# A transformer decoder layer on one core: new durations in the count of times that places the steps of a top-k search

## The chip, the cores and the metric

The kernel runs on one core of one Trainium2 chip. The metric is the device time of one execution in microseconds (us). The kernel before takes 1329.95 us, the median of three runs (1328.74 to 1334.31).

## What is computed

One decoder layer on 1024 tokens of 1024 channels. The steps that matter here, cut from the reference:

```
h    = x * (1 + scale1) + shift1                       # scale, shift, gate from c @ W_mod
q, k, v, u, iq, ik, iw = split(h @ W_in)
score = sum over 8 indexer heads of iw * relu(iq . ik / 8), causal
idx   = top_k(score, 256)                              # per query, the 256 best keys
attn  = softmax attention of 8 heads over the keys idx only
pool  = causal window means (2, 4, 8, 16) of u, minus u, then a small matmul
x = LayerNorm(alpha * x + gate1 * (concat(attn, pool) @ W_o))
x = LayerNorm(alpha * x + gate2 * SwiGLU(x * (1 + scale2) + shift2))
```

Queries are worked on in eight tiles of 128 (tile 0 to tile 7). Tile i looks at 128 (i + 1) keys. Tiles 0 and 1 have at most 256 keys and need no selection.

## The kernel before, in words

The layer runs in stages: modulation and indexer projection, indexer scores (tiles 2 to 7 in turn), projections of u (pooling), k and v, attention, W_o with the first norm, and the feed-forward part.

**The search.** The 256th best score of a row is found by bisection over the bits of the score (`bisect`). A search has a first pass over the score, then 15 steps on the high 16 bits (`search_v` or `search_a` with `bits` 15), a pass that prepares the low bits, 16 steps on the low bits, and last a few operations that turn the found threshold into a mask written over the score. Three searches run side by side. One is on VectorE, for tiles 7, 6 and 5 at once (`TILES_V`; its small columns are `colsD`, its keys `keysD` and `keys`, its waste output `junk`): one step is three counting passes of 1024, 896 and 768 elements and two tiny operations. Two are on ScalarE: one for tiles 4 and 3 (`junkA`), one for tile 2 (`junkB`), with columns `colsA`; their first passes, their change from high to low bits and their masks are on VectorE too.

**The projections beside it.** While the searches run, TensorE computes u in four groups (`u_take` copies a group from PSUM on ScalarE into `ub` and forms the window sums on VectorE and GpSimd, `u_split` forms `phi` on ScalarE and `plo` on VectorE, `u_pool` multiplies), then k in eight tiles (`take` copies on ScalarE and rotates on GpSimd, `k_transpose` transposes on TensorE into `kT`, copies the high part on ScalarE and subtracts the low part on VectorE, both into `kr`), then v in eight tiles. Weights of each are split into a high and a low part (`ws`): high on ScalarE, low on VectorE for two quarters and on GpSimd for the other two. `gate_fin` (`gr`) stands in the middle of v.

**Attention.** It goes from tiles 7 and 6 down. A unit is a pair of heads of one tile: scores on TensorE (`s`, from `kr` and the query operands `qab`), mask and row maximum on VectorE (`sm`, in the trace CUSTOM_DVE_ANT_0, in the order of the program ISA), exponential on ScalarE, reciprocal on VectorE, scaling on GpSimd, transposes on TensorE (`pT`), product with v (`o`). `need(i)` makes sure that the mask of tile i has been issued before its first use.

**What sets the order.** Engines run their own queues in order. In the stages with the search, VectorE, ScalarE and GpSimd keep the order in which the program issues (`PIN`). That order is made by a count of times: each engine is wrapped in a `Queue`, which adds the assumed duration of each instruction (`cost`) to its own clock and notes when each buffer is written and read (`Times`). Before an instruction goes out, `fill` asks when its operands would be ready; if a waiting search step with its announced duration (the number after `yield`) ends by then plus a slack of 0.3 us (VectorE) or 0.4 us (ScalarE), the step goes out first. Steps that found no place are issued when `need` asks for the mask. No assumed duration reaches the chip except through this order. Behind the projections, VectorE, ScalarE and TensorE are ordered by the framework's scheduler, which does not read these durations.

Of the kernel before, what the change touches and what calls it, by code (L numbers as in the profile page):

```python
# [131 lines left out]
class Queue:  # L132
# [6 lines left out]
    def cost(self, op, out, k):  # L139
        n = 1  # L140
        for s_ in out.shape[1:]:
            n *= s_
        if self.name == "T":
            return 0.107 if op == "transpose" else max(n, 60) / 2400
        if self.name == "A":
            return max(0.19, 0.05 + n * 0.00088) + (0.09 if "accum_out" in k else 0)
        if self.name == "G":
            return 0.12 + n * {"tensor_tensor": 0.00225, "scalar_tensor_tensor": 0.0014}.get(op, 0.00125)
        if out.dtype in (BF16, I16, U16) and op in ("tensor_scalar", "tensor_tensor", "tensor_copy"):
            return 0.07 + n * (0.00065 if "accum_out" in k or op == "tensor_tensor" else 0.0003)  # L150
        return 0.07 + n * (0.00053 if op == "tensor_scalar" else 0.00106)

    def __getattr__(self, op):
        f = getattr(self.eng, op)
# [26 lines left out]
def decoder_layer_kernel(  # L181
# [8 lines left out]
    V, A, G, T, SP = (Queue(tc, e, n, pinned, times) for e, n in  # L190
                      ((nc.vector, "V"), (nc.scalar, "A"), (nc.gpsimd, "G"), (nc.tensor, "T"), (nc.sync, "S")))
# [448 lines left out]
    def bisect(tiles, cols, on_act):  # L640

        nt = len(tiles)
# [6 lines left out]
        def trash(i):  # L649
            return (ja if on_act else junkd(i))[:, 0 : P * (i + 1)]  # L650
# [10 lines left out]
        for m, i in enumerate(tiles):  # L661
            n = P * (i + 1)
# [8 lines left out]
        sum_w = sum(w_(i) for i in tiles)  # L671

        def search_v(bits, base, low):
            V.memset(cand, float(1 << (bits - 1)))
            for b in range(bits - 1, -1, -1):
                yield "V", 0.35 + 0.72 * sum_w
                for m, i in enumerate(tiles):
                    dt = U16 if low else I16
                    V.tensor_scalar(trash(i).bitcast(dt), kv[i].bitcast(dt), one(cand, m), one(base, m),
                                    ALU.is_ge, ALU.add, accum_out=one(cntc, m))  # L680
                V.tensor_scalar(pr, cntc, 0.0, float(1 << b), ALU.is_ge, ALU.mult)
                off = -float(1 << (b - 1)) if b > 0 else -1.0
                V.scalar_tensor_tensor(cand, pr, off, cand, ALU.add, ALU.add)

        def search_a(bits, low):

            V.memset(cand, 0.5 - float(1 << (bits - 1)))
            for b in range(bits - 1, -1, -1):
                yield "A", 1.0 * sum_w + 0.65 * nt
                for m, i in enumerate(tiles):  # L690
                    A.activation(trash(i), kv[i].bitcast(U16 if low else I16), AF.Sign, bias=one(cand, m),
                                 accum_out=one(cntc, m))

                for m in range(nt):
                    A.activation(one(pr, m), one(cntc, m), AF.Sign, bias=one(thr, m))
                for m in range(nt):
                    A.activation(one(cand, m), one(pr, m), AF.Identity, scale=-0.5 * float(1 << b), bias=one(cand, m))
            yield "V", 0.1
            V.tensor_scalar(cand, cand, -1.0, None, ALU.mult)

        yield from (search_a(15, False) if on_act else search_v(15, kp, False))
        V.tensor_copy(M, cand)
        for m, i in enumerate(tiles):
            yield "V", 1.8 * w_(i)
            V.tensor_scalar(trash(i).bitcast(I16), kv[i], one(M, m), one(kp, m), ALU.is_gt, ALU.add,
                            accum_out=one(ng, m))
            lv = score(i).bitcast(U16).rearrange("p (n two) -> p n two", two=2)
            V.scalar_tensor_tensor(kv[i].bitcast(U16), kv[i], one(M, m), lv[:, :, 0], ALU.is_equal, ALU.mult)
            if on_act:
                V.tensor_scalar(one(thr, m), one(ng, m), 2.0, float(P * (i + 1) + 1), ALU.mult, ALU.add)  # L710
        yield from (search_a(16, True) if on_act else search_v(16, ng, True))

        V.tensor_copy(ib.bitcast(I32), M)
# [4 lines left out]
        for m, i in enumerate(tiles):  # L718
            n = P * (i + 1)
# [66 lines left out]
    for i in range(2, NT):  # L786
# [3 lines left out]
        n = P * (i + 1)  # L790
# [970 lines left out]
    for p in range(1, NFP):  # L1761
        n_of = {"g": 0, "d": 0, "u": 0}
        for kind in DOWN_AT if p < NFP - 1 else "g" * 7 + "u" * 7:
            n = n_of[kind]
# [134 lines left out]
```

## Time and profile before

| what | value |
|---|---|
| median of three runs | 1329.95 us |
| the profiled execution | 1327.57 us, its span 1325.8 us |
| mean granted TensorE clock | 0.955 |
| TensorE (PE) busy | 1186.7 us, 90% |
| VectorE (DVE) busy | 1070.5 us, 81% |
| ScalarE (ACT) busy | 642.7 us, 48% |
| GpSimd (POOL) busy | 709.2 us, 53% |

Shares over the whole span mix stages with different limits. The searches lie between about 126 and 415 us of the span, so the stretches of that time have to be read one by one. All instructions of wrapped engines carry line 168, which is a helper's, so rows are told apart by the names of their buffers.

### The profile page before, as it was taken

To read this page: it belongs to the slowest core of one execution; us is meant where nothing else is said; L and a number is where in the kernel's file an instruction comes from. 1 tells how busy PE (TensorE), PEld (TensorE's weight loads), DVE (VectorE), ACT (ScalarE), POOL (GpSimd) and SP (SyncE) were. 2 spreads that over 40 slices of the span, in tenths; PEclk is the share of its full clock that TensorE was granted. 3 is DMA by queue.
4 is the path that set the end of the run, shared out by engine and by line. 5 is a ranking of instruction groups with operands and counts; after the bars stand their busy time and mean duration, and the time that the engine had idled before them with its cause. 6 is when DMAs were issued, how large, how long until landed. Compare 5 with 4: busy or idle time off the path is not lost.

```text
span 1325.8 us, 16034 instructions
## 1 busy us (share of the span) xinstructions
PE 1186.7 (90%) x5462; PEld 927.9 (70%) x5462; DVE 1070.5 (81%) x1769; ACT 642.7 (48%) x1335; POOL 709.2 (53%) x495
## 2 busy tenths in 40 slices
PE   7979996858749997999689999999999999999996
PEld 6646585646536654788577787878787887878775
DVE  6898999999997698576687787776868777777698
ACT  3345794847857776535544343333334333333531
POOL 1392463535003354428677384765748475576848
PEclk9999998979878998999899999999999999999998
DMA  9540020301100166420020101102120111113113
GB/s 341 225 158 26 17 96 17 111 33 48 41 16 9 57 215 239 148 84 9 32 96 32 64 33 64 64 32 80 39 73 32 64 36 61 64 47 112 43 60 120
DMA packets 34904, 103.91 MB, mean 78 GB/s; under 512 B 3843, under 2 KB 3843, under 8 KB 33286
## 3 DMA queue, kind: packets, MB, share of 16 engines
q1 hardware_dynamic: 34822, 102.88, 22.3%
q8 instruction: 43, 0.70, 0.2%
q14 instruction: 39, 0.32, 0.1%
HBM read 93.42 MB, written 9.45 MB: 78 GB/s over the span
## 4 chain that ended last, share of the span: by engine, by line
PE 37%; DVE 6%; POOL 4%; issue 2%; ACT 1%; DVEq 0%; POOLq 0%; ACTq 0%
PE gu L168 23%; PE dn L168 14%; DVE act_W L168 2%; POOL wraw_R L168 2%; DVE utmp_X L168 1%; POOL wraw_W L168 1%; DVE gtmp_V L168 1%; POOL wblk_V L168 1%; POOL wblk_T L168 0%; DVE wblk_T L168 0%; DVE hr_H L168 0%; POOL hr_H L168 0%; DVE wblk_V L168 0%; DVE res_X L168 0%; DVE stat_C L168 0%
## 5 line engine op out<-in xcount | busy, mean ns | idle before, releaser
L168 PE MATMUL gu<-hr_H,wblk_V 128*128 128x512 f32 (+1 forms) x924 | 215.7, 385 | 4.3 <-POOL wblk_V L168 2.1
L168 PE MATMUL gu<-hr_H,wblk_T 128*128 128x512 f32 (+1 forms) x924 | 215.6, 385 | 3.6 <-POOL wblk_T L168 1.9
L168 PEld LDWEIGHTS gu<-hr_H,wblk_V 128*128 128x128 f32 x924 | 169.9, 188 | 41.3 <-POOL wblk_V L168 4.2
L168 PEld LDWEIGHTS gu<-hr_H,wblk_T 128*128 128x128 f32 x924 | 170.5, 188 | 39.9 <-POOL wblk_T L168 3.6
L168 DVE TENSOR_TENSOR res_X<-res_X,dn 128x512 f32<-128x512 f32 (+1 forms) x253 | 158.9, 677 | 15.4 <-PE dn L168 15.3
L168 POOL TENSOR_SCALAR sm_H<-sm_H,stat_X 128x1024 f32<-128x1024 f32 (+7 forms) x64 | 57.2, 907 | 139.0 <-DVE stat_X L168 127.8
L168 PE MATMUL pj<-ws_W,hT_H 128*128 128x512 f32 x456 | 122.0, 416 | 10.5 <-DVE kr_K L168 5.4
L168 POOL TENSOR_TENSOR wraw_R<-wraw_R 128x512 f32<-128x512 f32 x64 | 94.3, 1481 | 47.0 <-DVE wblk_T L168 23.7
L168 POOL TENSOR_TENSOR wraw_W<-wraw_W 128x512 f32<-128x512 f32 x60 | 86.7, 1452 | 57.9 <-DVE wblk_V L168 29.3
L168 PEld LDWEIGHTS pj<-ws_W,hT_H 128*128 128x128 f32 x456 | 87.0, 197 | 37.7 <-issue 15.5
L168 PE MATMUL dn<-wblk_T,act_W 128*128 128x512 f32 x324 | 78.8, 391 | 4.5 <-DVE act_W L168 4.5
L168 PE MATMUL dn<-wblk_V,act_W 128*128 128x512 f32 x324 | 78.5, 391 | 2.9 <-DVE act_W L168 2.5
L168 DVE TENSOR_SCALAR_CACHE_REDUCE junk_X<-keysD_T,colsD_X 128x1024 int16<-128x1024 int16 (+1 forms) x64 | 78.9, 1269 | 0.7
L168 ACT ACTIVATE wblk_V<-wraw_R 128x512 fp32r<-128x512 f32 x56 | 35.3, 630 | 81.0 <-POOL wraw_R L168 62.6
L168 PEld LDWEIGHTS dn<-wblk_T,act_W 128*128 128x128 f32 x324 | 60.4, 188 | 19.0 <-DVE act_W L168 6.6
L168 PEld LDWEIGHTS dn<-wblk_V,act_W 128*128 128x128 f32 x324 | 60.4, 188 | 17.4 <-DVE act_W L168 4.2
L168 ACT ACTIVATE wblk_V<-wraw_W 128x512 fp32r<-128x512 f32 x53 | 33.1, 628 | 75.0 <-POOL wraw_W L168 56.4
L168 ACT ACTIVATE wblk_T<-wraw_W 128x512 fp32r<-128x512 f32 x56 | 35.0, 628 | 65.9 <-POOL wraw_W L168 50.2
L168 POOL TENSOR_TENSOR ws_W<-raw_R,ws_W 128x1024 fp32r<-128x1024 f32 x11 | 30.8, 2797 | 63.2 <-ACT ws_W L168 63.2
L168 ACT ACTIVATE wblk_T<-wraw_R 128x512 fp32r<-128x512 f32 x52 | 32.5, 627 | 60.9 <-POOL wraw_R L168 45.5
L168 POOL TENSOR_TENSOR ptmp_C<-rope_V,gr_G 128x512 f32<-128x512 f32 x16 | 25.8, 1610 | 66.1 <-ACT rope_V L168 65.7
L168 ACT ACTIVATE sm_H<-sm_H,stat_X 128x1024 f32<-128x1024 f32 (+7 forms) x64 | 49.1, 768 | 23.4 <-DVE stat_X L168 23.1
(298 smaller groups left out, 2785.6 us busy)
## 6 DMA issues: line engine op xcount, KB each, us to landing
wm_K<-in_wma_dram SPq DMA_DIRECT2D x16, 512.0 KB, 9.9
modraw_V<-in_wmc_dram SPq DMA_DIRECT2D x16, 512.0 KB, 4.5
wraw_R<-in_wg_dram SPq DMA_DIRECT2D x6, 1024.0 KB, 4.7
wraw_R<-in_wd_dram SPq DMA_DIRECT2D x12, 512.0 KB, 3.6
wraw_W<-in_wup_dram SPq DMA_DIRECT2D x12, 512.0 KB, 3.6
modraw_V<-in_wmg_dram SPq DMA_DIRECT2D x10, 512.0 KB, 4.3
wraw_R<-in_wup_dram SPq DMA_DIRECT2D x10, 512.0 KB, 3.5
wraw_W<-in_wg_dram SPq DMA_DIRECT2D x5, 1024.0 KB, 4.7
```

The costliest lines, as they stand in the source:

```text
L168: ins_ = f(*a, **k)
```

## The change

The assumed durations of instructions on TensorE, ScalarE and VectorE are replaced, and so are the announced durations of a search step. For the VectorE search (three tiles, summed width 2.625) a step was announced as 0.35 + 0.72 * 2.625 = 2.24 and is now announced as 0.4 + 1.08 * 2.625 + 0.35 * 3 = 4.29. No instruction is added or taken away and no operand changes; the order of VectorE, ScalarE and TensorE changes, that of GpSimd and of the DMA queue does not.

```diff
         if self.name == "T":
-            return 0.107 if op == "transpose" else max(n, 60) / 2400
+            return 0.13 if op == "transpose" else max(n * 0.000443, 0.11)
         if self.name == "A":
-            return max(0.19, 0.05 + n * 0.00088) + (0.09 if "accum_out" in k else 0)
+            return max(0.26, 0.14 + n * 0.00088) + (0.31 if "accum_out" in k else 0)
...
         if out.dtype in (BF16, I16, U16) and op in ("tensor_scalar", "tensor_tensor", "tensor_copy"):
-            return 0.07 + n * (0.00065 if "accum_out" in k or op == "tensor_tensor" else 0.0003)
-        return 0.07 + n * (0.00053 if op == "tensor_scalar" else 0.00106)
+            if "accum_out" in k:
+                return 0.35 + n * 0.00105
+            return 0.07 + n * (0.00065 if op == "tensor_tensor" else 0.0003)
+        return max(0.16, 0.07 + n * (0.00053 if op == "tensor_scalar" else 0.00106))
...
-                yield "V", 0.35 + 0.72 * sum_w
+                yield "V", 0.4 + 1.08 * sum_w + 0.35 * nt
...
-                yield "A", 1.0 * sum_w + 0.65 * nt
+                yield "A", 0.9 * sum_w + nt
```

**First place: VectorE where the first key tiles get their low parts.** `kr` is the key operand, `kT` the transposed key tile in PSUM, `junk` with `colsD` a search step. In the kernel before:

```order
L168 TENSOR_SCALAR junk_X_607,colsD_X_615<-keysD_T_610,colsD_X_615 128x1024
L168 TENSOR_SCALAR junk_X_608,colsD_X_615<-keysD_T_610,colsD_X_615 128x896
L168 TENSOR_SCALAR junk_X_609,colsD_X_615<-keys_T_612,colsD_X_615 128x768
L168 TENSOR_SCALAR colsD_X_615<-colsD_X_615 128x3
L168 SCALAR_TENSOR_TENSOR colsD_X_615<-colsD_X_615 128x3
L168 TENSOR_TENSOR kr_K_1231<-kT_1990,kr_K_1231 64x4x128 x2
L168 TENSOR_TENSOR kr_K_1231<-kT_2021,kr_K_1231 64x4x128 x2
```

The same place in the changed kernel, with the ScalarE searches' change to the low bits (`colsA`, `keysA`) and the next weight split:

```order
L170 TENSOR_TENSOR kr_K_1225<-kT_1849,kr_K_1225 64x4x128 x2
L170 TENSOR_SCALAR junkA_T_613,colsA_X_606<-keysA_X_605,colsA_X_606 128x512
L170 SCALAR_TENSOR_TENSOR keysA_X_605<-keysA_X_605,colsA_X_606,score_X_77 128x512
L170 TENSOR_SCALAR colsA_X_606<-colsA_X_606 128x1
L170 MEMSET colsA_X_606 128x2
L170 TENSOR_TENSOR kr_K_1225<-kT_1924,kr_K_1225 64x4x128 x2
L170 TENSOR_TENSOR kr_K_1225<-kT_1946,kr_K_1225 64x4x128 x2
L170 TENSOR_TENSOR kr_K_1225<-kT_1990,kr_K_1225 64x4x128 x2
L170 TENSOR_TENSOR ws_W_69<-raw_R_75,ws_W_69 128x1024
```

The search steps that stood between the key tiles before are gone from between the first four.

**Second place: VectorE around the gate row in the middle of v.** `gr` is the gate, `gt` its PSUM tile. In the kernel before:

```order
L168 TENSOR_SCALAR junk_X_607,colsD_X_615<-keysD_T_610,colsD_X_615 128x1024
L168 TENSOR_SCALAR junk_X_608,colsD_X_615<-keysD_T_610,colsD_X_615 128x896
L168 TENSOR_SCALAR junk_X_609,colsD_X_615<-keys_T_612,colsD_X_615 128x768
L168 TENSOR_SCALAR colsD_X_615<-colsD_X_615 128x3
L168 SCALAR_TENSOR_TENSOR colsD_X_615<-colsD_X_615 128x3
L168 TENSOR_TENSOR gr_G_76<-raw_R_73,gt_2386 128x512
L168 TENSOR_TENSOR gr_G_76<-raw_R_73,gt_2399 128x512
```

The same place in the changed kernel; the rows that write `keysD` and `keys` from `score` are the search's change from high to low bits:

```order
L170 TENSOR_TENSOR gr_G_76<-raw_R_73,gt_2266 128x512
L170 SCALAR_TENSOR_TENSOR keysD_T_610<-keysD_T_610,colsD_X_615,score_X_77 128x1024
L170 TENSOR_TENSOR gr_G_76<-raw_R_73,gt_2274 128x512
L170 TENSOR_SCALAR junk_X_608,colsD_X_615<-keysD_T_610,colsD_X_615 128x896
L170 TENSOR_SCALAR junk_X_609,colsD_X_615<-keys_T_612,colsD_X_615 128x768
L170 SCALAR_TENSOR_TENSOR keysD_T_610<-keysD_T_610,colsD_X_615,score_X_77 128x896
L170 SCALAR_TENSOR_TENSOR keys_T_612<-keys_T_612,colsD_X_615,score_X_77 128x768
L170 MEMSET colsD_X_615 128x3
```

Before, 29 of the 31 steps stand ahead of the gate and 2 behind it; now 15 stand ahead of it and all 16 steps on the low bits behind it, along with most of the preparation of the low bits.

**Third place: VectorE at the first attention unit.** ISA is the masked row maximum of a head. In the kernel before:

```order
L168 TENSOR_SCALAR keys_T_611<-score_X_77,colsA_X_606 128x640
L168 TENSOR_SCALAR junkA_T_613,colsA_X_606<-score_X_77,colsA_X_606 128x640
L168 TENSOR_SCALAR keysA_X_605<-score_X_77,colsA_X_606 128x512
L168 TENSOR_SCALAR colsA_X_606<-colsA_X_606 128x1
L168 TENSOR_TENSOR qab_H_2528<-qT_2535,qab_H_2528 64x512
L168 SCALAR_TENSOR_TENSOR score_X_77<-keys_T_611,colsA_X_606 128x640
L168 TENSOR_TENSOR qab_H_2528<-qT_2535,qab_H_2528 64x512
L168 TENSOR_SCALAR score_X_77<-score_X_77 128x640
L168 TENSOR_TENSOR qab_W_2529<-qT_2540,qab_W_2529 64x512 x2
L168 ISA sm_H_2527,stat_X_2522<-s_2619,score_X_77 128x1024
```

And in the changed kernel:

```order
L170 TENSOR_SCALAR score_X_77<-junk_X_607 128x1024
L170 TENSOR_SCALAR keys_T_611<-score_X_77,colsA_X_606 128x640
L170 TENSOR_SCALAR junkA_T_613,colsA_X_606<-score_X_77,colsA_X_606 128x640
L170 TENSOR_SCALAR keysA_X_605<-score_X_77,colsA_X_606 128x512
L170 TENSOR_SCALAR colsA_X_606<-colsA_X_606 128x1
L170 ISA sm_H_2390,stat_X_2385<-s_2452,score_X_77 128x1024
L170 ISA stat_X_2385 128x1
L170 SCALAR_TENSOR_TENSOR score_X_77<-keys_T_611,colsA_X_606 128x640
```

The masks of tiles 7, 6 and 5 were complete ahead of the first ISA; now only that of tile 7 is, the ends of the others follow between the ISA rows of the first units, and the four operations on `qab` stand earlier, among the low steps.

## Rows read from the trace of the kernel before

**Rows 1.** Stretches: length, busy us (instructions) of PE, PEld, DVE, ACT, POOL, clock, DMA:
```profile
189.60:369.40 179.80, 133.92 (x546) 106.01 (x545) 173.04 (x318) 118.27 (x332) 57.98 (x39) 0.88 0.15 50
369.40:394.70 25.30, 9.57 (x36) 6.06 (x34) 24.74 (x46) 13.99 (x37) 0.00 (x0) 0.67 0.07 21
394.70:430.00 35.30, 33.25 (x177) 21.49 (x178) 28.93 (x65) 26.00 (x54) 12.81 (x12) 0.80 0.03 8
```
**Rows 2.** Timeline of DVE: start us, us, operation, idle before it:
```profile
202.73 1.34 DVE L168 TENSOR_SCALAR_CACHE_REDUCE junk_X<-keysD_T,colsD_X 128x1024 int16<-128x1024 int16 x1
...
206.63 1.34 DVE L168 TENSOR_SCALAR_CACHE_REDUCE junk_X<-keysD_T,colsD_X 128x1024 int16<-128x1024 int16 x1
...
216.66 1.22 DVE L168 TENSOR_TENSOR plo_V<-ub_V,phi_V 128x1024 fp32r<-128x1024 f32 x1 [1.12 <-ACT phi_V L168]
...
229.35 1.23 DVE L168 TENSOR_TENSOR plo_V<-ub_V,phi_V 128x1024 fp32r<-128x1024 f32 x1 [1.13 <-ACT phi_V L168]
...
244.47 2.85 DVE L168 TENSOR_TENSOR ub_V<-ub_V 128x1024 f32<-128x1024 f32 x1 [0.50 <-ACT ub_V L168]
247.66 1.23 DVE L168 SCALAR_TENSOR_TENSOR ub_V<-ub_V,ub_V 128x1024 f32<-128x1024 f32 x1 [0.34 <-POOL ub_V L168]
```
**Rows 3.** Timeline of PE: start us, us, operations, idle before them:
```profile
172.83 11.12 PE L168 MATMUL pair<-hT_H,ws_W 128*128 128x512 f32 x48
...
217.16 1.22 PE L168 MATMUL po<-phi_V,wps_X 128*128 128x512 f32 x2 [11.46 <-ACT ub_V L168]
...
292.09 1.09 PE L168 MATMUL kT<-const_C,rope_V 128*128 128x128 f32 x4 [15.76 <-DVE kr_K L168]
...
326.14 5.61 PE L168 MATMUL pj<-ws_W,hT_H 128*128 128x512 f32 x24
...
361.14 12.68 PE L168 MATMUL pj<-ws_W,hT_H 128*128 128x512 f32 x48 [2.71 <-DVE gr_G L168]
...
404.78 3.67 PE L168 MATMUL pT<-const_C,sm_H 128*128 128x128 f32 x16
```
**Rows 4.** Timeline of ACT:
```profile
188.77 0.81 ACT L168 ACTIVATE junkA_T<-keys_T,colsA_X 128x640 bf16<-128x640 int16 x1
...
191.17 0.81 ACT L168 ACTIVATE junkA_T<-keys_T,colsA_X 128x640 bf16<-128x640 int16 x1
...
215.57 1.06 ACT L168 ACTIVATE phi_V<-ub_V 128x1024 fp32r<-128x1024 f32 x1 [15.85 <-DVE ub_V L168]
...
293.22 1.19 ACT L168 ACTIVATE kr_K<-kT 64x512 fp32r<-64x512 f32 x2 [13.36 <-PE kT L168]
```
**Rows 5.** Timeline of POOL:
```profile
198.60 6.35 POOL L168 TENSOR_TENSOR ub_V<-ub_V 128x1024 f32<-128x1024 f32 x3 [7.74 <-DVE ub_V L168]
...
237.16 2.87 POOL L168 TENSOR_TENSOR ws_W<-raw_R,ws_W 128x1024 fp32r<-128x1024 f32 x1 [3.18 <-ACT ws_W L168]
```
**Rows 6.** Timeline of DVE at the end of the search:
```profile
369.41 0.17 DVE L168 CAST colsD_X<-colsD_X 128x3 int32<-128x3 f32 x1
...
393.24 1.39 DVE L168 TENSOR_TENSOR qab_W<-qT,qab_W 64x512 fp32r<-64x512 f32 x2
394.66 1.23 DVE L168 CUSTOM_DVE_ANT_0 sm_H<-s,score_X 128x1024 f32<-128x1024 f32 x1
```
**Rows 7.** DVE groups from 189.5 to 369.4: count, busy us, mean ns, idle before:
```profile
L168 DVE TENSOR_TENSOR ws_W<-raw_R,ws_W 128x1024 fp32r<-128x1024 f32 x4 | 8.8, 2202 | 0.1
L168 DVE TENSOR_SCALAR colsD_X<-colsD_X 128x3 f32<-128x3 f32 (+1 forms) x32 | 8.7, 271 | 1.0
L168 DVE TENSOR_TENSOR ub_V<-ub_V 128x1024 f32<-128x1024 f32 x4 | 6.5, 1629 | 0.5 <-ACT ub_V L168 0.5
...
L168 DVE TENSOR_TENSOR plo_V<-ub_V,phi_V 128x1024 fp32r<-128x1024 f32 x4 | 4.9, 1221 | 2.3 <-ACT phi_V L168 2.2
```
**Rows 8.** Timeline of ACT and of DVE in the indexer scores:
```profile
144.04 0.61 ACT L168 ACTIVATE junkB_X<-keysA_X,colsA_X 128x384 bf16<-128x384 int16 x1 [3.11 <-DVE colsA_X L168]
...
163.63 2.67 DVE L168 SCALAR_TENSOR_TENSOR score_X<-relu_K,const_C,score_X 128x1024 f32<-128x1024 f32 x2 [0.55 <-ACT relu_K L168]
167.36 3.53 DVE L168 SCALAR_TENSOR_TENSOR score_X<-relu_K,const_C,score_X 128x1024 f32<-128x1024 f32 x2 [1.05 <-ACT relu_K L168]
```

## The prediction

> **What bounds the kernel now.** I first read the busy time by stretch, since shares of the whole span say little here. From 189.6 to 369.4 us, where the VectorE search runs beside the projections, VectorE is busy 173.0 of 179.8 us and TensorE 133.9 [rows 1]. So VectorE is the bound of that stretch and TensorE follows it. TensorE's timeline says the same from the other side: its long waits there, 11.46 us ahead of the first pooling product, 15.76 us ahead of the third key transpose and 2.71 us ahead of the last v tiles, all end with VectorE (the first by way of ScalarE's `phi`, which waits 15.85 us for VectorE) [rows 3, 4]. VectorE's own timeline shows how little it waits: four waits of 1.12, 1.13, 0.50 and 0.34 us, 3.1 us in all; the rest of the gap to 179.8 are short pauses between dependent tiny operations [rows 2]. The search ends at 369.41, the masks follow, and the first softmax operation starts at 394.66 [rows 6]. From 394.7 on TensorE is busy 33.25 of 35.3 us [rows 1]: the bound changes over to TensorE there. The time at which attention gets going is therefore set by VectorE: by the work that stands ahead of it, which is the same set of instructions in both kernels, plus VectorE's waits.
>
> **The change part by part.** A step of the VectorE search takes 3.90 us (206.63 minus 202.73) [rows 2]. Counted in the order, 29 of 31 steps stood ahead of the gate row and now 15 do. So 14 steps, 14 x 3.90 = 54.6 us, leave the projections and stand behind them, where nothing else is left for VectorE. For TensorE that is a gain: a group of 24 matmuls takes 5.61 us and 48 take 11.12 us [rows 3], and with its VectorE waits gone it should end the projections about 50 us earlier, near 322 instead of 373.8 us (361.14 + 12.68) [rows 3]. That gain is worth nothing by itself, since attention then stands still until the search is done. What counts is whether VectorE still has no waits while it paces nobody. It does not: with fewer steps to fill in, it waits for the others.
>
> I walked VectorE's new order from 189.6 us with the durations of the rows, against TensorE's, ScalarE's and GpSimd's new orders. The waits I find, with what ends them:
> - pooling, first group: 1.1 us for `phi`, as in the row before [rows 2].
> - second group: ScalarE now has three steps of its two-tile search (2.40 us each, 191.17 minus 188.77 [rows 4]) and the copies of the pooling product ahead of `phi`, so VectorE waits 2.7 us for it, and 0.4 us for GpSimd's sums.
> - first quarter of the k weights: one ScalarE step lies ahead of the copy, 2.0 us.
> - last two pooling groups: 0.3 us behind a GpSimd weight split of 2.87 us [rows 5] and 0.8 us for `phi`.
> - k tiles 0 to 3 have no step between them any more: VectorE needs 0.7 us for each half tile (1.39 for two such operations [rows 6]), TensorE 5.61 us for a tile's projection, ScalarE 1.19 us for the copy ahead of it [rows 3, 4]. Waits of 0.4 and 2.8 us.
> - k tiles 4 to 7, with the wait for the one-tile search's ScalarE part: 1.3, 2.5, 2.8 and 0.9 us.
> Sum: 1.1 + 3.1 + 2.0 + 1.1 + 3.2 + 7.5 = 18.0 us, against 3.1 us before. The ends of this term: 8 us if ScalarE and TensorE run ahead of my walk by a step each time, 25 us if each wait is a ScalarE step longer.
>
> Four operations on `qab`, 0.69 us each [rows 6], move from behind the search into it: +2.8 us for the search's end, and the same less behind it.
>
> Collisions with GpSimd take from this. The same kind of operation takes 1.22 us where GpSimd is quiet (`plo`) and 2.20 and 1.63 us on the mean for the weight splits and the window sums; the tiny `colsD` operation takes 0.27 us on the mean [rows 7] against 0.17 for the like one at the search's end [rows 6]. That excess is 4 x 0.98 + 4 x 0.41 + 32 x 0.10 = 8.8 us, with the like on other tiny operations some 11. GpSimd's work is unchanged, and in my walk two of its four weight splits meet VectorE again. I take 4 us as saved, out of a range from 0 to 11. The Trainium skill weighs in here: its page "SBUF — State Buffer", section "SBUF: two separate sides", says that a VectorE operation with two SBUF inputs and a GpSimd operation contend for one port pair, an exclusive lock, so that the loser is held for the other's whole instruction. By that rule a VectorE operation that starts during a 2.87 us split waits up to all of it, or not at all if it starts elsewhere; the rows agree in kind (2.85 us for one sum instead of 1.22 [rows 2]), and the rule alone would allow this term to go to zero or to all 11 us.
>
> The search's end then moves by 18.0 - 3.1 + 2.8 - 4 = +13.7 us, from 369.4 to about 383.
>
> Behind the search: the mask of tile 7 alone stands ahead of the first softmax operation, so that starts about 15 us behind the search's end instead of 25.25 us (394.66 minus 369.41) [rows 6]. But some 10 us of the other masks now stand between the two heads of the second unit and ahead of the first reciprocal, without which no transpose starts. Before, the first transposes start 35.4 us behind the search's end (404.78 minus 369.41) [rows 3, 6]; adding up the new order with the rows' durations I come to 34.4 us. So nothing is won there. TensorE's granted clock is low in both restarts: 0.67 and 0.80 in the stretches from 369.4 and 394.7 [rows 1]. Now TensorE stands nearly still for some 70 us ahead of it and does its first scores with pauses, so I add 1.5 us (0 to 4) for work that before ran after the clock had risen.
>
> In the indexer scores three ScalarE steps fewer stand among the relus. ScalarE waits 3.11 us there for a search column, and VectorE waits 0.55 and 1.05 us for relus [rows 8]. VectorE is busy there as well, so I take -1 us (0 to -2.7). What follows attention's start keeps its order, and its transfers are issued by the same instructions, so it only shifts.
>
> Sum: 13.7 + 1.5 - 1 = +14.2 us. On the profiled execution, 1327.57 us, that gives 1341.8. That execution lies 2.4 us under the median of the runs, so the median after could be up to that much higher; I say 1342.
>
> **The rivals.**
> First, not slower: the collisions go instead of the waits. Place: the weight splits, window sums and tiny operations from 189.6 us on. If VectorE's waits are spent where GpSimd would have held it anyway, all 11 us of excess go, not 4, and the score stretch gives its full 2.7: 18.0 - 3.1 + 2.8 - 11 + 1.5 - 2.7 = +5.5, 1333 us, within what can be told from no change. It decides from about 9 us saved on. For it: 2.20 against 1.22 us. Against it: GpSimd's list is the same, and the key rotations now lie closer to VectorE's work.
>
> Second, faster: the waits that I count do not come up, because ScalarE gets to `phi` and the key copies earlier than I have it (TensorE no longer lags, so ScalarE is released sooner everywhere). Place: pooling and k. With waits as before (3.1), 2.8 for `qab`, 11 us of collisions gone, 2.7 from the scores: -10.9, 1317 us. It needs VectorE free of waits while TensorE alone paces the key tiles; it decides once the waits are under about 5 us. Against it: between k tiles 0 and 3 VectorE has only 6 us of work for 22 us of TensorE's, and the steps ahead of that are fixed by the order.
>
> Third, slower still: no collisions saved and a cold restart, 18.0 - 3.1 + 2.8 + 4 = +21.7, 1349 us.
>
> That the change does nothing is excluded by the changed order.
>
> **How the numbers follow.** Half a per cent, 6.6 us, is about what a measurement of this kernel can tell from no change. The forecast with its own range of 1335 to 1349 has 0.70, and a small part of it (0.04) lies under 1336.6. The first rival has 0.15, the second 0.09, the third 0.06. Faster: 0.09. Same: 0.15 + 0.04 = 0.19. Slower: 0.66 + 0.06 = 0.72. The range that should hold the time 8 times in 10 reaches from the first rival's better half, 1331, to the third, 1350.
>
> **What would show it right or wrong.** Right: TensorE ends the v projection near 322 us, VectorE's search ends between 380 and 388, its timeline shows waits for `phi`, `ws` and `kr` of some 15 to 20 us, TensorE is nearly idle from 325 to 395, and all that follows is shifted by the same amount. Wrong: a search that ends before 375 us, few waits on VectorE, or a time of the feed-forward part that differs. If the search ends late and the total does not follow, then attention's start had room that I have not seen.

## The result and the profile after

The changed kernel takes 1341.93 us, the median of four runs (1340.49 to 1342.97), against 1329.72 us before, now the median of four. The ratio is 1.0081, with a 95% interval of 1.006 to 1.0102: slower by 12.2 us. The forecast was 1342.0. The profiled execution took 1342.97 us, its span is 1341.2 us (1325.8 before). One execution of e1 (2346 us) and one of the kernel before on the chip of e9 to e11 (6478 us) are left out of the figures below.

First the stretches of the kernel after (length, then busy us of PE, PEld, DVE, ACT, POOL, clock, DMA), which answer to [rows 1]: the search from the same start, the restart up to the first transposes of attention, and the whole from the first pass of VectorE's search to the first product with v.

```profile
189.60:387.01 197.41, 133.37 (x579) 106.01 (x577) 173.94 (x324) 138.98 (x393) 58.93 (x39) 0.84 0.13 46
387.01:419.62 32.61, 9.00 (x17) 4.00 (x17) 32.48 (x72) 4.95 (x9) 1.18 (x2) 0.50 0.00 0
173.25:429.19 255.94, 168.29 (x714) 130.81 (x713) 228.88 (x426) 164.53 (x454) 79.69 (x56) 0.81 0.13 46
```

The last of these in the kernel before:

```profile
173.32:414.79 241.47, 177.81 (x713) 136.57 (x713) 229.98 (x417) 161.00 (x443) 78.52 (x56) 0.84 0.14 49
```

VectorE's work in it is nearly the same (229.98 and 228.88 us). What it is not busy went from 241.47 - 229.98 = 11.5 to 255.94 - 228.88 = 27.1 us. That is the loss in one line: +15.6 us of VectorE standing, -1.1 us of work. VectorE's timeline after (start, us, operation, idle before it) names the waits; in [rows 2] there were four of 3.1 us in all, here there are twelve of 19.6 us, of which seven, and then the search's end and the first softmax operation:

```profile
215.42 1.23 DVE L170 TENSOR_TENSOR plo_V<-ub_V,phi_V 128x1024 fp32r<-128x1024 f32 x1 [2.39 <-ACT phi_V L170]
...
219.73 1.23 DVE L170 TENSOR_TENSOR ws_W<-raw_R,ws_W 128x1024 fp32r<-128x1024 f32 x1 [1.95 <-ACT ws_W L170]
...
243.08 1.22 DVE L170 TENSOR_TENSOR plo_V<-ub_V,phi_V 128x1024 fp32r<-128x1024 f32 x1 [4.23 <-ACT phi_V L170]
...
269.74 1.39 DVE L170 TENSOR_TENSOR kr_K<-kT,kr_K 64x512 fp32r<-64x512 f32 x2 [1.18 <-ACT kr_K L170]
...
273.24 1.39 DVE L170 TENSOR_TENSOR kr_K<-kT,kr_K 64x512 fp32r<-64x512 f32 x2 [2.11 <-ACT kr_K L170]
...
286.80 1.39 DVE L170 TENSOR_TENSOR kr_K<-kT,kr_K 64x512 fp32r<-64x512 f32 x2 [3.51 <-ACT kr_K L170]
...
298.16 1.39 DVE L170 TENSOR_TENSOR kr_K<-kT,kr_K 64x512 fp32r<-64x512 f32 x2 [1.68 <-ACT kr_K L170]
...
386.84 0.17 DVE L170 CAST colsD_X<-colsD_X 128x3 int32<-128x3 f32 x1
...
400.93 1.23 DVE L170 CUSTOM_DVE_ANT_0 sm_H<-s,score_X 128x1024 f32<-128x1024 f32 x1
```

The search ends at 386.84 instead of 369.41 [rows 6], 17.4 us later. TensorE's timeline shows the other side, to be read against [rows 3]: v is through at 326.4, and TensorE stands twice until VectorE releases it.

```profile
232.43 7.55 PE L170 MATMUL pair<-ws_W,hT_H 128*128 128x512 f32 x23 [5.37 <-DVE ws_W L170]
239.81 0.63 PE L170 MATMUL po<-phi_V,wps_X 128*128 128x512 f32 x2
...
309.44 16.93 PE L170 MATMUL pj<-ws_W,hT_H 128*128 128x512 f32 x72
...
356.88 1.95 PE L170 MATMUL s<-kr_K,qab_H 64*128 64x512 f32 x4 [26.43 <-DVE qab_H L170]
402.31 2.13 PE L170 MATMUL s<-kr_K,qab_W 128*128 128x512 f32 x4 [43.48 <-DVE stat_X L170]
...
419.62 3.67 PE L170 MATMUL pT<-const_C,sm_H 128*128 128x128 f32 x16 [0.99 <-POOL sm_H L170]
```

The account of the 12.2 us, in three parts. From the search's first pass to its end it took 386.84 - 173.25 = 213.6 us, before 369.41 - 173.32 = 196.1: +17.5 us. The first transposes stand 32.8 us behind the search's end (419.62 - 386.84), 35.4 before: -2.6 us. From the first operation on tile 5's scores to the search's first pass it took 173.25 - 114.61 = 58.6 us, before 173.32 - 112.07 = 61.25: -2.6 us. VectorE's busy time between those two points hardly changed (53.5 us before, 53.2 now), but its waits for relus fell from 3.0 us (0.48, 0.52, 0.38 and the two in [rows 8]) to 0.25. Not every wait that went was a gain: one unbroken row stands where [rows 8] had two waits, but it takes 12.2 us, against 11.9 for the same seven operations with their waits before (159.02 to 170.89), because each now takes 1651 ns on the mean instead of 1406.

```profile
114.61 0.55 DVE L170 TENSOR_SCALAR score_X<-relu_K,const_C 128x640 f32<-128x640 f32 x1 [1.98 <-ACT relu_K L170]
...
159.75 12.18 DVE L170 SCALAR_TENSOR_TENSOR score_X<-relu_K,const_C,score_X 128x1024 f32<-128x1024 f32 x7
```

17.5 - 2.6 - 2.6 = 12.3 us, next to the 12.2 us between the medians. The profiled execution shows 15.4 us of span: it also reached tile 5 at 114.61 instead of 112.07 (the profiled executions of all kernels reach it between 112.0 and 115.1, also where the order up to there is the same), it took 0.4 us less from the first transposes to the first product with v, and 1.0 us more followed that product (1341.2 - 429.19 = 912.0, before 911.0). That the scores shrank because ScalarE's steps left them is not shown by itself: e2, which keeps four of the five steps there, comes to 59.0 us.

### The profile page after: what moved, and what is told of

It reads as the page before. It is cut to its first block, busy times and chain, and to the rows that moved or that the text cites. A ratio compares the mean times of both kernels' runs of the same rounds, so it can differ in the third digit from the quotient of the medians.

```text
span 1341.2 us, 16033 instructions
## 1 busy us (share of the span) xinstructions
PE 1179.1 (88%) x5462; PEld 923.1 (69%) x5462; DVE 1067.2 (80%) x1769; ACT 643.0 (48%) x1335; POOL 705.7 (53%) x495
## 4 chain that ended last, share of the span: by engine, by line
PE 51%; DVE 28%; POOL 7%; issue 6%; ACT 6%; DMA 2%; DVEq 0%; SPq 0%; POOLq 0%; ACTq 0%
PE gu L170 23%; PE dn L170 13%; DVE junk_X L170 6%; PE pj L170 3%; DVE score_X L170 3%; PE pT L170 2%; PE o L170 2%; PE wo L170 2%; DVE act_W L170 2%; POOL wraw_R L170 2%; PE s L170 2%; DVE utmp_X L170 1%; DVE hr_H L170 1%; DVE stat_C L170 1%; PE pair L170 1%
## 5 line engine op out<-in xcount | busy, mean ns | idle before, releaser
L170 PEld LDWEIGHTS gu<-hr_H,wblk_T 128*128 128x128 f32 x924 | 172.3, 191 | 42.4 <-POOL wblk_T L170 3.5
L170 DVE TENSOR_TENSOR res_X<-res_X,dn 128x512 f32<-128x512 f32 (+1 forms) x253 | 158.9, 677 | 15.4 <-PE dn L170 15.3
L170 PE MATMUL pj<-ws_W,hT_H 128*128 128x512 f32 x456 | 118.2, 406 | 2.5 <-DVE const_C L170 1.7
L170 PEld LDWEIGHTS dn<-wblk_V,act_W 128*128 128x128 f32 x324 | 60.4, 188 | 17.4 <-DVE act_W L170 4.2
L170 PE MATMUL s<-kr_K,qab_W 128*128 128x512 f32 (+5 forms) x96 | 24.2, 410 | 44.0 <-DVE stat_X L170 44.0
```

Of the source, the lines that this page charges most:

```text
L170: ins_ = f(*a, **k)
```

## The experiments

All ratios stand against the kernel before on the same chip, where its median was 1328.5 to 1330.4 us. "Rows ahead" counts the search rows of tile 7 ahead of the gate row in VectorE's order, of 32 (31 steps and the counting pass that prepares the low bits). "Begins" is the time of the search's first pass, "work" is VectorE's busy time from there to the first product with v, "standing" is, as above, the rest of that stretch. The three add up to the time of the first product with v.

| kernel | rows ahead | begins | VectorE's work | standing | median, us | ratio (95%) |
|---|---|---|---|---|---|---|
| before | 30 | 173.3 | 230.0 | 11.5 | 1329.72 | 1 |
| after | 16 | 173.3 | 228.9 | 27.1 | 1341.93 | 1.0081 (1.006 to 1.0102) |
| e1 | 18 | 172.7 | 225.5 | 29.4 | 1343.88 | 1.0099 (1.0081 to 1.0117) |
| e2 | 20 | 171.1 | 231.1 | 10.6 | 1327.2 | 0.9979 (0.9968 to 0.9989) |
| e3 | 31 | 170.0 | 232.1 | 14.5 | 1331.24 | 1.0008 (0.9999 to 1.0017) |
| e4 | 30 | 175.8 | 226.7 | 15.7 | 1338.1 | 1.0054 (1.0037 to 1.0071) |
| e9 | 20 | 172.3 | 231.7 | 10.7 | 1328.24 | 0.9982 (0.9969 to 0.9995) |
| e10 | 26 | 169.4 | 225.1 | 4.5 | 1314.81 | 0.9879 (0.9857 to 0.9902) |
| e11 | 22 | 169.3 | 224.1 | 8.1 | 1318.65 | 0.991 (0.9886 to 0.9934) |
| e12 | 32 | 170.4 | 229.0 | 15.9 | 1328.06 | 0.9984 (0.9973 to 0.9994) |

Standing alone does not order the kernels: e12 stands 4.4 us more than the kernel before and is no slower, since its search begins 2.9 us earlier; e4 loses most of its time behind the first product with v.

**One number alone (e1), the queue durations alone (e2).** The kernel before, with one part of the change each.

```diff
-                yield "V", 0.35 + 0.72 * sum_w
+                yield "V", 0.4 + 1.08 * sum_w + 0.35 * nt
```

> The kernel before, with only the announced length of a VectorE search step changed (2.24 to 4.29 us); the durations in the queues and ScalarE's steps keep their old numbers. In the order 18 search rows of tile 7 stand ahead of the gate row (32 in all; 30 before, 16 after), and the indexer scores keep their five small ScalarE steps. Theory (the loss is VectorE's new waits in the projections): nearly all of it comes from this one number. Waits on VectorE of about 12 to 15 us, search end near 382, nothing gained in the scores: about 1341 us (1336 to 1344). Rival (ScalarE's new numbers cost the time, because they move its steps out of the scores and ahead of phi and the key copies): no loss here, 1328 to 1332.

Ratio 1.0099: this number alone brings all of the loss. VectorE waits 22 us up to the search's end, more than the 12 to 15 that I forecast. The search ends at 394.54 and not near 382, but the masks of tiles 4, 3 and 2 stand ahead of that end here, so the end by itself misleads; the standing, 29.4 us, does not. The rival on ScalarE's numbers falls as the cause of this loss.

> The kernel before, with only the durations of single instructions in the queues changed; the announced lengths of search steps keep their old numbers. 20 of 32 search rows of tile 7 stand ahead of the gate row, four small ScalarE steps in the scores. Theory: some steps are put between the key tiles again, so waits of about 8 to 10 us on VectorE and a search end near 376: about 1335 us (1331 to 1339), between before and after. Rival (only the announced step length matters): 1328 to 1331. Rival (ScalarE's numbers cost the time): 1330 or less.

Ratio 0.9979, faster than forecast. I put its waits at 8 to 10 us from the gaps between the key rows; the trace has 6.0 us, and the restart is short, 399.66 - 373.05 = 26.6 us. The time also lies where the rival on ScalarE's numbers had put it; e9 below keeps ScalarE's new lengths, has 0.9982, and so decides against that rival.

**ScalarE's step lengths alone (e4).**

```diff
-                yield "A", 1.0 * sum_w + 0.65 * nt
+                yield "A", 0.9 * sum_w + nt
```

> The kernel before, with only the announced lengths of ScalarE's search steps changed. VectorE's order keeps 30 of 32 search rows ahead of the gate row; four small ScalarE steps in the scores instead of five. Theory: VectorE's waits stay near 3 us, and the scores gain 0 to 1 us: 1329 us (1326 to 1332). Rival (ScalarE's numbers cost the time): 1335 or more.

A miss: 7 us slower, though VectorE's order is nearly that of before. The search ends at 371.33 and the first product with v starts at 418.21, 3.4 us later than before, of which 2.5 are there when the search begins; another 8 us go behind it (1337.1 - 418.21 = 918.9, before 911.0; the other kernels lie between 910 and 916). ScalarE's timeline, then VectorE's, show what is different there: the two-tile search on ScalarE is not through when attention starts, its last steps stand among the exponentials, and VectorE makes the masks of tiles 4 and 3 in the middle of attention.

```profile
437.18 0.84 ACT L168 ACTIVATE junkA_T<-keys_T,colsA_X 128x640 bf16<-128x640 uint16 x1
```

```profile
442.54 0.87 DVE L168 TENSOR_SCALAR_CACHE_REDUCE junkA_T<-score_X,colsA_X 128x640 bf16<-128x640 f32 x1
```

That these masks cost the 8 us is my reading; no run tests it. In the kernel after, ScalarE's search is done by 357.2, so this is a second way to lose time and not the one of the change.

**The place of the steps (e3, e9, e10, e11, e12).** e3 and e10 are the kernel after with a larger slack, 6.0 and 4.0; e9 is after with the old announced step; e11 is e9 with a slack of 1.0; e12 is before with a slack of 2.0.

```diff
-SLACK = {"V": 0.3, "A": 0.4}
+SLACK = {"V": 4, "A": 0.4}
```

> The kernel after with all its new numbers, but VectorE's allowed delay by a search step (its slack) 6.0 instead of 0.3 us. 31 of 32 search rows of tile 7 stand ahead of the gate row, one search step between any two key operations. Theory: VectorE's waits fall back to under 6 us and the search ends near 370, with the whole of after's loss gone: about 1328 us (1323 to 1334; the upper end if VectorE then waits for ScalarE's search, which this order wants finished earlier). Rival (the loss is in the restart: TensorE stands still, the clock falls): TensorE is again slowed through the projections and busy until the search's end, so it gives the same time as the theory; told apart by TensorE's clock and the distance from the search's end to the first transposes, which the theory wants unchanged at 33 to 35 us. Rival (ScalarE's new numbers cost the time): about 1341.

VectorE has no wait at all up to the search's end; the loss of the kernel after is gone, but not more. The first transposes stand 32.9 us behind the search's end, 32.8 in the kernel after and 35.4 in the kernel before, so the restart is not where the loss lay. TensorE is now late: v and the query transposes end at 383.5, and behind the search VectorE waits for TensorE's scores, two of the waits being these.

```profile
382.47 1.03 PE L170 MATMUL qT<-const_C,raw_R 128*128 128x128 f32 x8
```

```profile
399.81 1.09 DVE L170 CUSTOM_DVE_ANT_0 sm_H<-s,score_X 128x896 f32<-128x896 f32 x1 [1.17 <-PE s L170]
...
404.20 1.23 DVE L170 CUSTOM_DVE_ANT_0 sm_H<-s,score_X 128x1024 f32<-128x1024 f32 x1 [1.20 <-PE s L170]
```

> The kernel after with the announced length of a VectorE search step put back (2.24 us); all other new numbers stay. 20 of 32 search rows of tile 7 stand ahead of the gate row (16 after, 30 before), none between the first six key operations, three small ScalarE steps in the scores. Theory (VectorE's waits from the scores to the first pooled output decide, at equal work): waits between the kernel with the queue durations alone and the kernel after, the score stretch as short as after's: 1332 us (1327 to 1336). Rival (ScalarE's step lengths cost the time, as they did alone): 1337 or more.

Ratio 0.9982: with the one number put back the whole change is a little faster than before, at the lower end of my range. ScalarE's lengths cost nothing in this company.

> The kernel after with VectorE's slack at 4.0 instead of 0.3 us: 26 of 32 search rows ahead of the gate row, five small ScalarE steps in the scores, a search step between nearly all pairs of key operations. Theory: VectorE's waits near 5 us and TensorE not yet late for the first scores (it was at slack 6, 31 rows): 1326 us (1322 to 1331), so at least as fast as before. Rival (more rows ahead of the gate row make TensorE late at once): 1331 or more.

Ratio 0.9879, 16 us faster than before, better than my range, and the fastest of all: a version that beats both kernels. The search ends at 358.63, the first transposes stand 29.9 us behind it, and between 188 and the search's end VectorE waits once, 0.33 us. The stretch, the group of VectorE's weight splits (count, busy us, mean ns, idle before) and the restart:

```profile
169.39:399.01 229.62, 175.81 (x718) 136.30 (x716) 225.13 (x415) 163.13 (x447) 76.35 (x56) 0.85 0.16 52
```

```profile
L170 DVE TENSOR_TENSOR ws_W<-raw_R,ws_W 128x1024 fp32r<-128x1024 f32 x6 | 7.3, 1220 | 0.1
```

```profile
388.54 3.67 PE L170 MATMUL pT<-const_C,sm_H 128*128 128x128 f32 x16 [3.00 <-POOL sm_H L170]
```

Its first product with v comes 15.8 us earlier than before (399.01 against 414.79), and less than half of that is standing: 7.0 us less standing, 4.9 less work, and a search that begins 3.9 us earlier. The work shrank mainly because the six weight splits take 7.3 us together, in the kernel before 13.6 (11.3 for the five inside its stretch). Part of the earlier beginning is that one of these splits, of 2.3 us before, now follows the first pass.

> The kernel after with the old announced length of a VectorE step and a slack of 1.0 us: 22 of 32 search rows ahead of the gate row, one step between every two key operations from the first pair on, four small ScalarE steps in the scores. Theory: waits of about 7 us on VectorE, 1327 us (1323 to 1332). Rival (the number of rows behind the gate row is what counts, not the waits): 10 rows behind it, so about two thirds of after's loss, 1336 or more.

Ratio 0.991, faster than I said. Ten rows stand behind the gate row, against two before, and it is still 12 us faster, so the number of steps left behind does not decide. Nor is it standing alone: the first product with v comes 13.3 us earlier than before, by 3.4 us less standing, 5.9 less work and a search that begins 4.0 us earlier.

> The kernel before with all its old numbers and VectorE's slack at 2.0 instead of 0.3 us: all 32 search rows of tile 7 stand ahead of the gate row, 23 of them ahead of the first key operation (17 before, 15 with the new numbers and slack 4). Theory (attention starts when VectorE is through and TensorE has not been held back past that): VectorE waits for nobody up to the search's end, but TensorE is late and VectorE waits for it behind the search, as at slack 6 with the new numbers: 1333 us (1329 to 1338). Rival (a larger slack alone wins, whatever the announced durations): 1320 or less.

1328.06, just under my range; the mechanism is that of e3, with v and the query transposes through at 392.2 and VectorE waiting behind the search, 3.4 us for ScalarE's copy of the queries, then 1.0 to 2.3 us at a time for TensorE's scores and transposes. A slack of 2.0 alone does not win; with the old durations no smaller one was run.

**Less work in the search (e5, e6).** Four of the 31 steps left out, in the kernel before and in the kernel after.

```diff
-            for b in range(bits - 1, -1, -1):
+            for b in range(bits - 1, 3 if low else -1, -1):
                 yield "V", ...
```

> The kernel before with the last four of the 31 steps of VectorE's search left out (the low four bits of the thresholds are not searched; 28 search rows of tile 7, all ahead of the gate row). Theory (attention starts when VectorE has done its work plus its waits, in both kernels): VectorE waits little here, so its end moves by nearly all of 4 x 3.90 = 15.6 us, to 1315 us (1312 to 1320). Rival (TensorE, which this kernel holds back through the projections, sets attention's start as much): at most half of it, 1322 or more.

1319.79 us, ratio 0.9925 (0.9906 to 0.9943): some 10 us of 15.6, between the two. VectorE's work in the stretch falls by 14.6 us (215.42 of 229.00 us), its standing rises by 2.1 us, and the row for that is not TensorE but ScalarE's search:

```profile
380.33 0.17 DVE L168 TENSOR_SCALAR colsA_X<-colsA_X 128x2 f32<-128x2 f32 x1 [2.15 <-ACT colsA_X L168]
```

So the kernel before has little room left on its other engines. Some 2 us more went in the indexer scores of the profiled execution (63.4 instead of 61.25 us; e4 has 63.5), for which I have no cause.

> The kernel after with the same four steps left out; they fall out of the stretch behind the projections, where TensorE stands still (12 search rows instead of 16 behind the gate row). Theory: the whole 15.6 us, 1326 us (1324 to 1329), so that the distance to the kernel before with the same cut stays near 12 us. Rival (the distance comes from the restart or from ScalarE's search, not from VectorE's waits): less than 10 us gained, 1332 or more, and ScalarE's search would end later than VectorE's.

1322.45 us, ratio 0.9948 (0.9934 to 0.9963): below my range. By the two ratios that is 17.7 us less than the kernel after, 2 more than the steps are worth. The stretch became 233.56 us, 22.4 shorter: 19.2 us of work, more than the 15.6 of the steps because other operations now stand behind the first product with v (375 instructions instead of 426, where four steps are 32), and 3.2 us of standing. The distance to e5 is 2.7 us and not 12, so that part of the expectation fell. It rested on equal work, and the stretches of e6 and then e5 do not have that: e6 stands 10.3 us more, but has 5.7 us less work, and in these executions its search begins 7.4 us earlier.

```profile
171.10:404.66 233.56, 167.90 (x709) 130.18 (x709) 209.73 (x375) 161.56 (x450) 80.31 (x56) 0.83 0.15 50
178.46:407.46 229.00, 178.50 (x713) 137.44 (x712) 215.42 (x385) 160.73 (x443) 78.57 (x56) 0.85 0.15 51
```

**TensorE kept at work (e7, e8).** 480 and 400 transposes ahead of attention's scores, on the kernel after and on e2.

```diff
     for i in (7, 6):
         q_make(i, qr[i], qp[i])
+    warm2 = psA("warm2")
+    for _ in range(480):
+        T.transpose(warm2[:, 0:P], ident, ident)
```

> The kernel after with 480 transposes of a constant put on TensorE between the query transposes and the first attention scores, where it stands still; at about 0.125 us each they end near 388 us, ahead of the search's end plus the first mask. They keep its granted clock up (in the kernel after it is 0.50 from 360 to 400 and 0.69 from 400 to 440). My forecast put 1.5 us (0 to 4) on the cold restart. Theory (VectorE paces the restart): 0 to 2 us won, 1340 to 1342. Rival (the clock is a main part of the loss): 4 us or more won, under 1338. Should the transposes run at the lower clock, they overrun the search and the time rises by 20 us or more.

> The kernel with only the durations of single instructions changed (1327.2 us, a little faster than before), with 400 such transposes at the same place. Its granted clock is 0.50 from 360 to 400. Theory: 0 to 2 us won, 1325 to 1327. Rival (the clock is a main part): under 1324.

Both were slower and outside every forecast: 1346.87 us (ratio 1.0142, 1.0119 to 1.0164) and 1337.34 us (1.0062, 1.0047 to 1.0076). The transposes did not overrun. The rows of e7 show what happened instead:

```profile
325.58 52.56 PE L170 MATMUL warm<-const_C 128*128 128x128 f32 x480
377.90 1.83 PE L170 MATMUL s<-kr_K,qab_H 128*128 128x512 f32 x8
415.32 4.22 PE L170 MATMUL s<-kr_K,qab_W 128*128 128x512 f32 x8 [35.59 <-DVE stat_X L170]
```

```profile
385.33 0.17 DVE L170 CAST colsD_X<-colsD_X 128x3 int32<-128x3 f32 x1
...
413.94 1.23 DVE L170 CUSTOM_DVE_ANT_0 sm_H<-s,score_X 128x1024 f32<-128x1024 f32 x1
```

With them the order changed: the masks of all six tiles stand ahead of the first softmax operation, 28.6 us behind the search's end instead of 14.1 (in e8 31.0 instead of 12.6). So the two runs do not test the clock alone; I take the place of the masks for the main part of the loss, which no run separates: 1346.87 against 1341.93 us on the kernel after, 1337.34 against 1327.2 us on e2. The price of the clock stays open: TensorE stood again from 379.7 on, and its granted clock was back at 0.50 in this stretch of e7.

```profile
390.00:400.00 10.00, 0.00 (x0) 0.00 (x0) 10.00 (x21) 0.00 (x0) 0.00 (x0) 0.50 0.00 0
```

## Why the prediction was right, and where its terms were not

**The mechanism.** The bound was read rightly: attention starts when VectorE is through, and TensorE's 50 us are worth nothing. I said v near 322 us, a search end between 380 and 388, waits of 15 to 20 us and a TensorE nearly idle from 325 to 395; it was 326, 386.8, 19.6, and one stand of 43.48 us behind one of 26.43. e1 and e9 show that the announced step of VectorE's search carries the loss, e11 that steps left behind need not cost time.

**The waits, 18.0 us forecast, 19.6 measured.** Most terms were within 0.5 us: 2.7 for the second group was 2.39, 2.0 for the k weights 1.95, 3.2 for the first k tiles 3.29. The other k tiles, with a wait for weights, had 7.5 and took 6.3. One was mis-sized: 0.8 us for the last `phi` was 4.23. I took ScalarE's place in the order and left out that the pooled product ahead of `phi` waits behind a group of TensorE, which itself waited 5.37 us for VectorE's weight split (232.43 in the rows above). ScalarE's copies of that product, which stand ahead of `phi`, show the wait:

```profile
240.71 1.39 ACT L170 ACTIVATE pout_K<-po,const_C 128x512 f32<-128x512 f32 x2 [7.49 <-PE po L170]
```

VectorE waited for its own lateness, by way of TensorE and ScalarE. Some 1.85 us of that lateness is an operation ahead of the split that took 2.02 us instead of 0.17 beside a GpSimd split (last section).

**The collisions, -4 forecast.** The stretch from the search's first pass to its end grew by 17.5 = 19.6 - 3.1 + 2.8 + x, so x = -1.8. VectorE's busy time says the same: up to the end of the search's last conversion, before and then after, it goes from 189.42 to 190.22 us, +0.8, of which `qab` is +2.8, so -2.0 for the rest.

```profile
173.32:369.58 196.26, 150.38 (x618) 119.57 (x618) 189.42 (x336) 132.88 (x375) 71.92 (x50) 0.89 0.17 57
173.25:387.01 213.76, 149.72 (x651) 119.49 (x650) 190.22 (x340) 152.62 (x432) 72.86 (x50) 0.86 0.16 55
```

The groups from 189.5 to 387, to be read against [rows 7], say where: weight splits and first window sums got shorter by 1.5 and 1.6 us, but the pass that ends a window sum, which took 1220 ns before, now takes 1768 and gives back 2.2. Some 1.8 us more come from tiny operations, among them one on `colsA` of 128x2 that went from 1.28 to 0.16; the remaining +0.7 is spread thinly over the others.

```profile
L170 DVE TENSOR_SCALAR colsD_X<-colsD_X 128x3 f32<-128x3 f32 (+1 forms) x32 | 9.1, 286 | 1.0
L170 DVE TENSOR_TENSOR ws_W<-raw_R,ws_W 128x1024 fp32r<-128x1024 f32 x4 | 7.3, 1828 | 2.2 <-ACT ws_W L170 2.1
L170 DVE SCALAR_TENSOR_TENSOR ub_V<-ub_V,ub_V 128x1024 f32<-128x1024 f32 x4 | 7.1, 1768 | 0.6 <-POOL ub_V L170 0.3
...
L170 DVE TENSOR_TENSOR ub_V<-ub_V 128x1024 f32<-128x1024 f32 x4 | 4.9, 1220 | 0.0
```

The first rival's price was real all the same: in e10 all six splits run at 1220 ns.

**The restart, +1.5 forecast.** It was -2.6. My own sum had come to 34.4 us instead of 35.4, and I set that 1.0 at nothing; it is 32.8, so the masks' place was worth more than I had added up. Nothing shows that the lower clock cost more than before: the first 16 transposes take 3.67 us in both. In e2 the granted clock is 0.50 from the search's end to the first transposes, as in the kernel after, and that stretch is shorter than before and the kernel no slower.

```profile
373.22:399.66 26.44, 8.64 (x16) 3.79 (x17) 26.30 (x50) 8.39 (x21) 1.63 (x2) 0.50 0.00 0
```

**The scores, -1 forecast,** were -2.6, the end of my range. So four terms were off, by +1.6, +2.2, -4.1 and -1.6: together -1.9, which is 14.2 less 12.3. The agreement with the median is luck in two ways: the errors nearly cancel, and I added 14.2 to the profiled execution of 1327.57. Added to the median of 1329.95 it would have been 1344.1, 2.2 us more than measured.

**The rivals.** The first (collisions gone, about 1333) fell, since the collisions moved. The second (few waits, 1317) is what e10 does, by another slack. The third's collisions (none saved) were as near as mine, but its cold restart did not come.

**Why a truer number is slower.** A step may go in if it ends by its announced length within the slack. A real step is 3.90 us [rows 2], so the real overshoot that the rule allows is slack + 3.90 - announced: 0.3 + 3.90 - 2.24 = 1.96 us before, 0.3 + 3.90 - 4.29 = -0.1 us after. The old number was wrong and contained a slack. With the new queue durations, the ratio falls with the overshoot and then rises again: -0.1 gives 1.0081, 1.96 (e9) 0.9982, 2.7 (e11) 0.991, 3.6 (e10) 0.9879, 5.6 (e3) 1.0008. The best of the five lies where VectorE hardly stands and TensorE is not yet late. With the old queue durations 3.7 us (e12) puts all 32 rows ahead and gives 0.9984. At about that overshoot the truer durations (e10, 0.9879) are worth 1%, which the change as made hides. Whether the old durations with a smaller overshoot would do as well was not run.

## What to carry to other kernels

Count when the bounding engine begins a stage, what it does and what it stands, up to the event that starts the next one. In these runs a moved step cost time where it left a gap behind or made another engine late for that event. When a planner's numbers are corrected, look for a margin that the wrong number contained, and tune the margin again before judging the numbers.

## What the runs showed of the hardware

A tiny VectorE operation can lengthen beside a GpSimd operation as a large one does. The kernel after has one on 128x3 elements that took 2.02 us, where the like take 0.17:

```profile
227.88 2.02 DVE L170 TENSOR_SCALAR colsD_X<-colsD_X 128x3 f32<-128x3 f32 x1
```

It ended at 229.90, and GpSimd's weight split beside it at 227.53 + 2.34 = 229.87:

```profile
227.53 2.34 POOL L170 TENSOR_TENSOR ws_W<-raw_R,ws_W 128x1024 fp32r<-128x1024 f32 x1 [4.14 <-ACT ws_W L170]
```

The Trainium skill, "SBUF — State Buffer", section "SBUF: two separate sides", says that the one of VectorE and GpSimd that comes second to their shared ports is held until the other's instruction ends. By these two rows the trace agrees. The page names for it VectorE operations in a 2-port mode or with two SBUF inputs; which of the two this one would be, no run here shows.
